# Seven instead of eight seven-product pairs in the second down projection of a decoder layer's first feed-forward block

## The chip, the cores and the metric

The kernel runs on one core of one Trainium2 chip. The metric is the time on the device in microseconds, from the launch of the program to its end; lower is better. A profiled execution gives, beside its own time, the span of the recorded instructions.

## The reference

One layer of a decoder, all in float32, for 256 tokens of width 2048. A feed-forward block (width 5632) stands before and behind a mixing stage of two head groups:

```python
def swiglu(x, w_gate, w_up, w_down):
    return (jax.nn.silu(x @ w_gate) * (x @ w_up)) @ w_down

def reference(x, ...):
    for l in range(DEPTH):          # DEPTH = 1
        x = x + 0.5 * swiglu(rms_norm(x, ffn1_norm[l]), ffn1_w_gate[l], ffn1_w_up[l], ffn1_w_down[l])
        h = rms_norm(x, mix_norm[l])
        z = h @ w_in[l]
        ...                         # gated linear attention and dilated attention
        x = x + jnp.concatenate([o_g, o_a], axis=-1) @ w_out[l]
        x = x + 0.5 * swiglu(rms_norm(x, ffn2_norm[l]), ffn2_w_gate[l], ffn2_w_up[l], ffn2_w_down[l])
    return x
```

The diff touches the last product of the first `swiglu`, the down projection: 256 x 5632 times 5632 x 2048.

## The kernel before, in words

**Precision.** TensorE multiplies fp32r numbers. Every float32 operand is split in two: a high part, which ScalarE copies (`split`, L115), and a low part, which VectorE subtracts (L116). A product is then three matmuls: high by high (L279 or L304), high by low weight (L281 or L305), low activation by high weight (L283 or L306). Each has a stationary block of 128 x 128 activations and streams 512 columns of weights.

**Columns, k-tiles and pairs.** The 2048 columns of the down projection's result are made in two goes of 1024 (`cp` 0 and 1); a go is called a column pair, or down pair here. It sums over 44 k-tiles of 128, taken two at a time as 22 k-pairs. The weights of a k-pair are one tile `raw` of 1 MB, one load on SP's queue (L221), with three buffers. The split weights `wh` and `wl` have four buffers each, and `weights()` prepares up to two tiles ahead of the one that it hands out.

**Plain and seven pairs.** A plain k-pair is two units, one for each k-tile: per unit two halves of the tokens, two halves of the columns and three matmuls, so 12, and 24 for the pair. Its weights are two splits of 128 x 1024. A seven pair computes the same 2 x 2 blocks (tokens) by 2 x 2 blocks (k by columns) with seven block products in place of eight, as Strassen's and Winograd's scheme does: 21 matmuls (`seven_products`). For that VectorE first adds up sums of the weight blocks (`seven`: L243, L244, L247) and splits them; its weights take three splits of 128 x 1024 and one of 128 x 512. It also needs sums of the activations (`seven_forms`: L322 twice, L325 to L328, a split), made once per k-pair and column pair where they are not kept from the column pair before. Plain products add into the banks `cs`, seven products into both `cs` and four more banks `ms`.

**The order.** `DOWN_ORDERS` holds for each column pair a text of 22 letters, s for plain and g for seven; `_order` numbers the seven pairs first, so that seven pairs are k-pairs 0, 1, 2 and so on. `seven_pair` walks through the units. Forms of the seven pairs 0 to 5 are made during the first column pair; those of 6 and 7 are made in the second one, at units 13 and 16 (`extra`), in rooms that pairs 1 and 2 have done with (`dforms`, parts of `hh` and `hl`). At the last seven pair the banks `ms` are folded into `xs` by nine instructions (`fold_into_xs`, L425 to L432), one for each following half unit (a half unit is one half of the tokens, 6 matmuls). At the end of a column pair `evac` adds the plain banks into `xs` (L531).

**Work beside it.** The list `later` holds small pieces of other work that are strewn over the half units. In the second down pair these are the norm for the mixing stage: finished columns are turned by VectorE (L130), moved by DMAs that POOL issues (L137), multiplied with the gains (L157) and split into `hh` and `hl`. While the rooms there are lent to the seven pairs, the pieces from L157 on wait in the list `held`, which joins `later` at the last seven pair:

```python
if n == lastseven:
    folds = fold([...])
    if holding[0] == 1:
        later.extend(held)
        held.clear()
        holding[0] = total = done = step = 0
        steps = 2 * (len(units) - n) - 6
```

A planner then orders each engine's instructions from this program by its own estimate of times, so that the queue of VectorE need not follow the text; in the trace some L157 run ahead of the last seven pair. Both layers' feed-forward blocks are made by the same function `ffn`; the second layer's (`final`) has no norm behind it.

Of the kernel before, what the change touches and what calls it, by code (L numbers as in the profile page):

```python
# [39 lines left out]
def _order(text):  # L40

    seven, plain = iter(range(text.count("g"))), iter(range(text.count("g"), len(text)))
    return [(next(seven), True) if c == "g" else (next(plain), False) for c in text]


FF_ORDERS = [_order("ssgsggss" if b in FF_THREE else "ssgssgss" if b in FF_SEVEN else "ssssssss") for b in range(FF // 512)]
DOWN_ORDERS = [_order("ssssssgssgssgsgsgsgsss"), _order("sgsgsgsgsgsgsgssgsssss")]
OUT_ORDERS = [_order("ssssssss"), _order("ssgsgsss")]


def layer_kernel(tc, x, xT, gains, gla_gate_up, gla_gate_bias, gla_out_norm, att_q_norm, att_k_norm,
# [6 lines left out]
    with ExitStack() as es:  # L58
# [7 lines left out]
        def acc_bank():  # L66
            n = order[0]
            order[0] = (n + 1) % 6
            if n < 4:
                return pacc.tile([P, 512], F32, name="acc", tag="acc")  # L70
            return paux.tile([P, 512], F32, name="acc", tag="acc")

        def four_banks(odd):

            if odd:
                return [paux.tile([P, 512], F32, name="acc", tag="acc") for _ in range(2)] + [tp_bank() for _ in range(2)]
            return [pacc.tile([P, 512], F32, name="acc", tag="acc") for _ in range(4)]

        def t512(name):
            return cst.tile([P, 512], F32, name=name, tag="t512", bufs=4)  # L80

        def tp_bank():
            return ptp.tile([P, 512], F32, name="tp", tag="tp")
# [11 lines left out]
        hh = cst.tile([P, KT, S], F32R, name="hh")  # L95
        hl = cst.tile([P, KT, S], F32R, name="hl")
# [80 lines left out]
        def jobs_of(w, orders):  # L177
            for cp, order in enumerate(orders):
                for kp, seven in order:
                    for part in ("plain", "last", "sums", "more") if seven else (0, 1):  # L180
                        yield w, cp * len(order) + kp, part

        jobs = [*jobs_of(w_ff1, FF_ORDERS), *jobs_of(w_dn1, DOWN_ORDERS)]
        jobs += [(w_mix, i, k) for i in range(3 * KT // 2) for k in range(2)] + ["low"]
        jobs += [(w_mix, i, k) for i in range(3 * KT // 2, 3 * KT) for k in range(2)]
        jobs += jobs_of(w_out, OUT_ORDERS)
        jobs += [*jobs_of(w_ff2, FF_ORDERS), *jobs_of(w_dn2, DOWN_ORDERS)]

        AHEAD = 2
        ready = []  # L190
# [68 lines left out]
        def weights(early=False):  # L259
            if early:  # L260
                return prepare()
            while jobs and len(ready) <= AHEAD:
                prepare()
            return ready.pop(0)
# [5 lines left out]
        def halves(a):  # L270
            return a.rearrange("p (b a) -> p b a", b=2)

        def products(ps, t, acts, ws, first, last, js=((0, 1),)):
            for jj in js:
                for i, ((ah, al, k), (wh, wl)) in enumerate(zip(acts, ws)):
                    sh = ah[:, k, t * P:(t + 1) * P]
                    sl = al[:, k, t * P:(t + 1) * P]
                    for j in jj:
                        nc.tensor.matmul(ps[j], lhsT=sh, rhs=alt(wh[:, j, :]), start=first and i == 0, stop=False)  # L279
                    for j in jj:  # L280
                        nc.tensor.matmul(ps[j], lhsT=sh, rhs=alt(wl[:, j, :]), start=False, stop=False)  # L281
                    for j in jj:
                        nc.tensor.matmul(ps[j], lhsT=sl, rhs=alt(wh[:, j, :]), start=False, stop=last and i == len(ws) - 1)  # L283
# [5 lines left out]
        def run_later(n):  # L289
            for _ in range(min(n, len(later))):  # L290
                later.pop(0)()
# [39 lines left out]
        def seven_pair(acts, pairs, forms, odd, evac, fold, span=None, final=False, extra=None):  # L331

            cs, ms, folds = [acc_bank(), acc_bank(), tp_bank(), tp_bank()] if odd is None else four_banks(odd), None, []
            if odd is not None:
                order[0] = 4 * (1 - odd)
            units = [u for kp, seven in pairs for u in ([kp] if seven else [(2 * kp,), (2 * kp + 1,)])]
            lastseven = max(n for n, u in enumerate(units) if not isinstance(u, tuple))  # L340
            steps = span or 2 * sum(isinstance(u, tuple) for u in units)
            total = done = step = n = 0
            while n < len(units):
                u = units[n]
                if extra and n in extra:
                    extra[n]()
                if isinstance(u, tuple):
                    g = WBUF if final and n == len(units) - WBUF else 1
                    ws = [weights() for _ in range(g)]
                    last = n + g == len(units)  # L350
                    for t in range(NT):
                        step += 1
                        total = max(total, done + len(later))
                        go = min(max(-(-total * min(step, steps) // steps) - done, 0), len(later))
                        done += go
                        run_later(go)
                        if folds:
                            folds.pop(0)()
                        now = [acts[v[0]] for v in units[n:n + g]]
                        products(cs[2 * t:2 * t + 2], t, now, ws, n == 0, last, ((0,), (1,)) if g > 1 else ((0, 1),))  # L360
                        if last:
                            evac(t, [c.rearrange("p (a b) -> p b a", b=2) for c in cs[2 * t:2 * t + 2]])
                    n += g
                    continue
                start = ms is None
                if start:
                    ms = [acc_bank() for _ in range(4)] if odd is None else four_banks(1 - odd)
                seven_products(cs, ms, acts[2 * u:2 * u + 2], forms[u], start, n == lastseven)
                if start:
                    later.extend(second)  # L370
                    second.clear()
                if n == lastseven:
                    folds = fold([m.rearrange("p (a b) -> p b a", b=2) for m in ms])
# [5 lines that stand above are left out]
                n += 1  # L379
# [37 lines left out]
        def lent(a, k, i):  # L417

            return a[:, k:k + 2, :].rearrange("p k (t q) -> p (k t) q", q=P) if i else a[:, k:k + 2, :].rearrange("p k s -> p (k s)").unsqueeze(1)
# [15 lines left out]
        def ffn(name, done, residual, extra=None, final=False):  # L435

            with tc.tile_pool(name=name, bufs=1, reuse_waits="tile") as fp:
# [8 lines left out]
                def part(k):  # L446
                    n = int(k >= tail)
                    return us_h[n], us_l[n], k - n * tail
# [59 lines left out]
                dacts = [part(k) for k in range(FT)]  # L508

                rooms["down"] = {"sum": urs, "wh": lent(hl, 8, 0), "wl": lent(hl, 10, 0)}  # L510
                dforms = {kp + 1: [lent(hh, 2 * kp, 1), lent(hl, 2 * kp, 1)] for kp in range(4)}
                dforms[0] = [lent(hh, 12, 1), lent(hh, 14, 1)]
                dforms[5] = [lent(hl, 12, 1), lent(hl, 14, 1)]
                dforms.update({6 + i: [lent(a, 2 * i, 1) for a in (hh, hl)] for i in range(2)})

                def sums_of(kp):
                    seven_forms(dacts[2 * kp:2 * kp + 2], dforms[kp], t512("full"), t512("sums"))

                rest, later[:] = later[:], []
                for step in range(32):  # L520
                    kp = step // 5 - 1
# [4 lines left out]
                for cp in range(2):  # L526
                    def evac(t, ps, cp=cp):
                        for j in range(2):
                            c = 2 * cp + j
                            blk = xs[:, t, c * 512:(c + 1) * 512]  # L530
                            nc.vector.scalar_tensor_tensor(halves(blk), ps[j], 0.5, halves(blk), op0=ALU.mult, op1=ALU.add)  # L531
                            done(t, c, blk)

                    def fold(m, cp=cp):
                        return fold_into_xs(m, cp, urs, 0.5)

                    holding[0] = NT - cp
                    seven_pair(dacts, DOWN_ORDERS[cp], dforms, cp, evac, fold, span=28 if cp else 32, final=final and cp == 1,
                               extra={13 + 3 * i: lambda kp=6 + i: sums_of(kp) for i in range(2)} if cp else None)
                spare.close()  # L540


# [457 lines left out]
```

## Time and profile before

| what | value |
|---|---|
| median of 3 runs | 1709.99 us (1709.28 to 1711.11) |
| profiled execution, its own time | 1710.49 us |
| profiled execution, span | 1708.7 us |
| TensorE busy | 1696.9 us, 7932 matmuls |
| VectorE busy | 1472.8 us |
| ScalarE busy | 973.4 us |
| GpSimd busy | 506.2 us |
| granted TensorE clock | 0.999 |

The engines' names in the profile are PE (TensorE matmul), PEld (TensorE weight load, which overlaps PE), DVE (VectorE), ACT (ScalarE), POOL (GpSimd) and SP. A row of the order of instructions gives the start, the duration, engine, line, operation, tile written and tiles read, shape and count, and in brackets how long the engine had been idle and what released it. A row of a group gives line, engine, operation, tiles, shape and count, then the busy time in us and the mean of one in ns, then the idle time before them. The second down pair of the first layer runs from about 560 to 672 us of the span, that of the second layer from about 1594 to the end.

### The profile page before, as it was taken

The numbers are of one execution on the slowest core, as the hardware profiler recorded it, in microseconds if no ns is written. First come the engines' busy times: TensorE is split into PE (matmuls) and PEld (weight loads), VectorE is DVE, ScalarE is ACT, GpSimd is POOL, SyncE is SP. The second block draws the span as 40 slices with busy tenths as digits, with TensorE's granted clock in tenths as the row PEclk, the third lists the DMA queues.
The fourth block names the chain that finished last, engine by engine and source line by source line (L and its number), as shares of the span: only waits on it lengthen the run. The fifth ranks groups of instructions, "written<-read, shape, count | busy, mean of one in ns | idle before, by whom it ended". The sixth has DMA issues, their size and how long they took to land.

```text
span 1708.7 us, 22402 instructions
## 1 busy us (share of the span) xinstructions
PE 1696.9 (99%) x7932; PEld 1477.4 (86%) x7932; DVE 1472.8 (86%) x1823; ACT 973.4 (57%) x1207; POOL 506.2 (30%) x1002
## 2 busy tenths in 40 slices
PE   9999999999999999999999999999999999999999
PEld 7888888888888878888888888888888888888887
DVE  6989999999899997577856688989998999899986
ACT  7656565555555555564654555556555655555553
POOL 0333334343400601064250034333333333420000
PEclk9999999999999999999999999999999999999999
DMA  8566656666666666567564457666666666666663
GB/s 347 211 232 225 218 210 236 212 235 216 235 245 223 216 220 226 195 231 243 190 217 169 151 198 249 231 234 210 235 224 229 223 215 219 222 247 232 220 235 135
DMA packets 85809, 378.63 MB, mean 222 GB/s; under 512 B 21393, under 2 KB 38801, under 8 KB 42689
## 3 DMA queue, kind: packets, MB, share of 16 engines
q1 hardware_dynamic: 50864, 350.25, 57.9%
q0 software_dynamic: 34112, 25.88, 5.4%
q8 instruction: 62, 1.02, 0.2%
q10 hardware_dynamic: 720, 1.07, 0.2%
q14 instruction: 51, 0.41, 0.1%
HBM read 354.57 MB, written 4.19 MB: 210 GB/s over the span
## 4 chain that ended last, share of the span: by engine, by line
PE 89%; DVE 5%; DMA 4%; issue 1%; POOL 0%; ACT 0%; DVEq 0%; SPq 0%; ACTq 0%; POOLq 0%
PE acc L281 19%; PE acc L283 19%; PE acc L279 19%; PE acc L305 5%; PE acc L306 5%; PE acc L304 5%; PE tp L283 4%; PE tp L281 4%; PE tp L279 4%; DVE wl L116 3%; DMA raw<-in_w_dn_dram 2%; PE tp L306 1%; PE tp L305 1%; PE tp L304 1%; DMA xs<-us 1%
## 5 line engine op out<-in xcount | busy, mean ns | idle before, releaser
L115 ACT ACTIVATE wh<-raw 128x1024 fp32r<-128x1024 f32 (+2 forms) x610 | 631.9, 1047 | 444.0 <-PE acc L283 207.0
L116 DVE TENSOR_TENSOR wl<-raw,wh 128x1024 fp32r<-128x1024 f32 (+1 forms) x608 | 733.1, 1215 | 127.0 <-ACT wh L115 124.3
L137 POOL DMA_DIRECT2D xs<-us x704 | 344.5, 497 | 545.6 <-DVE us L130 284.1
L283 PE MATMUL acc<-wh,hl 128*128 128x512 f32 x1192 | 359.3, 381 | 0.0
L281 PE MATMUL acc<-wl,hh 128*128 128x512 f32 x1192 | 358.8, 381 | 0.1
L279 PE MATMUL acc<-wh,hh 128*128 128x512 f32 x1192 | 347.9, 381 | 2.3 <-ACT wh L115 2.3
L279 PEld LDWEIGHTS acc<-wh,hh 128*128 128x128 f32 x1192 | 224.8, 189 | 35.4 <-ACT wh L115 3.5
L281 PEld LDWEIGHTS acc<-wl,hh 128*128 128x128 f32 x1192 | 225.1, 189 | 32.7 <-DVE wl L116 0.5
L283 PEld LDWEIGHTS acc<-wh,hl 128*128 128x128 f32 x1192 | 225.3, 189 | 32.2 <-issue 0.5
L115 ACT ACTIVATE wh<-xs 128x1024 fp32r<-128x1024 f32 x100 | 105.6, 1056 | 103.3 <-DVE xs L247 31.9
L116 DVE TENSOR_TENSOR wl<-xs,wh 128x1024 fp32r<-128x1024 f32 x100 | 120.4, 1214 | 2.7 <-ACT wh L115 2.6
L281 PE MATMUL acc<-wl,uh 128*128 128x512 f32 x368 | 113.1, 381 | 2.6 <-DVE wl L116 2.6
L283 PE MATMUL acc<-wh,ul 128*128 128x512 f32 x368 | 112.2, 379 | 0.0
L279 PE MATMUL acc<-wh,uh 128*128 128x512 f32 x368 | 106.2, 380 | 0.5 <-ACT wh L115 0.5
L137 POOL DMA_DIRECT2D hh<-us x128 | 62.1, 500 | 121.1 <-DVE xs L531 68.5
L243 DVE TENSOR_TENSOR xs<-raw 128x1024 f32<-128x1024 f32 x50 | 61.1, 1222 | 29.3 <-DMA raw<-in_w_ff_dram 29.2
L281 PEld LDWEIGHTS acc<-wl,uh 128*128 128x128 f32 x368 | 68.7, 189 | 15.1 <-DVE wl L116 5.6
L279 PEld LDWEIGHTS acc<-wh,uh 128*128 128x128 f32 x368 | 69.3, 189 | 11.1 <-ACT wh L115 1.3
L283 PEld LDWEIGHTS acc<-wh,ul 128*128 128x128 f32 x368 | 69.6, 189 | 9.9
L279 PE MATMUL tp<-wh,hh 128*128 128x512 f32 x200 | 61.6, 379 | 0.0
L281 PE MATMUL tp<-wl,hh 128*128 128x512 f32 x200 | 59.5, 379 | 0.0
L283 PE MATMUL tp<-wh,hl 128*128 128x512 f32 x200 | 59.5, 379 | 0.0
(326 smaller groups left out, 2540.0 us busy)
## 6 DMA issues: line engine op xcount, KB each, us to landing
raw<-in_w_ff_dram SPq DMA_DIRECT2D x175, 1024.0 KB, 5.1
raw<-in_w_dn_dram SPq DMA_DIRECT2D x88, 1024.0 KB, 4.9
raw<-in_w_mix_dram SPq DMA_DIRECT2D x48, 1024.0 KB, 5.0
raw<-in_w_out_dram SPq DMA_DIRECT2D x16, 1024.0 KB, 4.8
xs<-us POOLq DMA_DIRECT2D x704, 16.0 KB, 4.0
xs<-in_x_dram SPq DMA_DIRECT2D x2, 1024.0 KB, 9.5
xs<-in_x_dram POOLq DMA_DIRECT2D x2, 1024.0 KB, 5.9
hh<-us POOLq DMA_DIRECT2D x128, 16.0 KB, 3.7
```

What stands on the lines that cost most here:

```text
L115: nc.scalar.activation(dst_h, src, AF.Copy)
L116: nc.vector.tensor_sub(dst_l, src, dst_h.bitcast(F32))
L137: nc.gpsimd.dma_start(dst[32 * q:32 * q + 32, ..., r * n:(r + 1) * n], src[32 * r:32 * r + 32, ..., q * n:(q + 1) * n])
L243: nc.vector.tensor_add(room["sum"], b1, blocks[:, 1:3, :])
L279: nc.tensor.matmul(ps[j], lhsT=sh, rhs=alt(wh[:, j, :]), start=first and i == 0, stop=False)
L281: nc.tensor.matmul(ps[j], lhsT=sh, rhs=alt(wl[:, j, :]), start=False, stop=False)
L283: nc.tensor.matmul(ps[j], lhsT=sl, rhs=alt(wh[:, j, :]), start=False, stop=last and i == len(ws) - 1)
L304: nc.tensor.matmul(bank, lhsT=a[0], rhs=alt(ws[0][:, j, :]), start=start, stop=False)
L305: nc.tensor.matmul(bank, lhsT=a[0], rhs=alt(ws[1][:, j, :]), start=False, stop=False)
L306: nc.tensor.matmul(bank, lhsT=a[1], rhs=alt(ws[0][:, j, :]), start=False, stop=stop)
```

## The change

The first layer's second down pair gets an order of its own. Before, both layers had `sgsgsgsgsgsgsgssgsssss`: eight seven pairs, mostly with one plain pair between two of them, and five plain pairs behind the last. Now the first layer has `sgsgssgssgssgssgssgsss`: seven seven pairs, the first two one plain pair apart, the others two, and three plain pairs behind the last. The units become 37 instead of 36, and the last seven pair is unit 30 instead of 25. The forms of k-pair 7 are no longer made in the first layer, since it is plain. The first down pair of both layers and everything of the second layer keep their text. The loop around the folds runs once, as the statement without it did.

```diff
-DOWN_ORDERS = [_order("ssssssgssgssgsgsgsgsss"), _order("sgsgsgsgsgsgsgssgsssss")]
+DOWN_ORDERS = {name: [_order("ssssssgssgssgsgsgsgsss"), _order(text)]
+               for name, text in (("ffn1", "sgsgssgssgssgssgssgsss"), ("ffn2", "sgsgsgsgsgsgsgssgsssss"))}
...
-        jobs = [*jobs_of(w_ff1, FF_ORDERS), *jobs_of(w_dn1, DOWN_ORDERS)]
+        jobs = [*jobs_of(w_ff1, FF_ORDERS), *jobs_of(w_dn1, DOWN_ORDERS["ffn1"])]
...
-        jobs += [*jobs_of(w_ff2, FF_ORDERS), *jobs_of(w_dn2, DOWN_ORDERS)]
+        jobs += [*jobs_of(w_ff2, FF_ORDERS), *jobs_of(w_dn2, DOWN_ORDERS["ffn2"])]
...
-                        if folds:
-                            folds.pop(0)()
+                        for _ in range(1):
+                            if folds:
+                                folds.pop(0)()
...
-                dforms.update({6 + i: [lent(a, 2 * i, 1) for a in (hh, hl)] for i in range(2)})
+                dforms.update({6 + i: [lent(a, 2 * i, 1) for a in (hh, hl)] for i in range(3)})
...
-                    seven_pair(dacts, DOWN_ORDERS[cp], dforms, cp, evac, fold, span=28 if cp else 32, final=final and cp == 1,
-                               extra={13 + 3 * i: lambda kp=6 + i: sums_of(kp) for i in range(2)} if cp else None)
+                    seven_pair(dacts, DOWN_ORDERS[name][cp], dforms, cp, evac, fold, span=28 if cp else 32, final=final and cp == 1,
+                               extra={at: lambda kp=6 + i: sums_of(kp) for i, at in enumerate((13,16,) if final else (13,))} if cp else None)
```

## The prediction

> **What bounds the kernel now.** I read the page first, then the engines' busy time by stretches, then the waits and the order of instructions around the second down pair of the first layer (called the stage below).
>
> ```profile
> span 1708.7 us, 22402 instructions
> PE   1696.9 (99%) x7932; PEld 1477.4 (86%) x7932; DVE 1472.8 (86%) x1823; ACT 973.4 (57%) x1207; POOL 506.2 (30%) x1002
> PE 89%; DVE 5%; DMA 4%; issue 1%; POOL 0%; ACT 0%; DVEq 0%; SPq 0%; ACTq 0%; POOLq 0%
> ```
>
> TensorE (PE) carries 89% of the chain that ended last, VectorE (DVE) 5%. So time falls by fewer matmuls, or by taking away a place where PE waits for weights. The change adds matmuls, so only waits are to be won. The stretches show whether the stage has any. Its ends are two like instructions: the first L531 after the pair before it, and the first L531 at its own end. Each was released by the same point of a pair (the first half of the tokens of its last k-tile), so the distance between them is one whole pair. The columns of the rows that begin with a stretch are its length and the busy time of PE, PEld, DVE, ACT and POOL, with clock, DMA share and GB/s last.
>
> ```profile
> 559.82 0.69 DVE L531 SCALAR_TENSOR_TENSOR xs<-acc,xs 128x512 f32<-128x512 f32 x1 [0.42 <-PE acc L283]
> 672.04 0.69 DVE L531 SCALAR_TENSOR_TENSOR xs<-acc,xs 128x512 f32<-128x512 f32 x1 [1.36 <-PE acc L283]
> 559.80:672.00 112.20, 109.82 (x505) 94.85 (x505) 99.44 (x118) 62.65 (x74) 35.50 (x72) 1.00 0.67 223
> 600.00:640.00 40.00, 37.62 (x171) 31.64 (x170) 37.43 (x45) 22.27 (x26) 1.72 (x4) 1.00 0.62 220
> 640.00:672.00 32.00, 32.00 (x150) 28.03 (x149) 23.79 (x27) 15.96 (x17) 4.44 (x8) 1.00 0.71 243
> 1600.00:1640.00 40.00, 40.00 (x187) 35.04 (x186) 34.88 (x37) 24.77 (x27) 0.00 (x0) 1.00 0.60 213
> ```
>
> PE is idle for 2.38 us between 600 and 640 and nowhere else in the stage, at a granted clock of 1.00 throughout. The last row is the same place of the second layer, whose second down pair runs the same order of pairs: no idle time. What PE waited for:
>
> ```profile
> 601.74 0.30 PEld L281 LDWEIGHTS acc<-wl,uh 128*128 128x128 f32 x2 [1.14 <-DVE wl L116]
> 612.82 0.30 PEld L281 LDWEIGHTS acc<-wl,uh 128*128 128x128 f32 x2 [1.51 <-DVE wl L116]
> 623.34 0.30 PEld L281 LDWEIGHTS acc<-wl,uh 128*128 128x128 f32 x2 [0.93 <-DVE wl L116]
> 633.32 0.30 PEld L281 LDWEIGHTS acc<-wl,uh 128*128 128x128 f32 x2 [0.40 <-DVE wl L116]
> ```
>
> Four times, some 10.5 us apart (one seven pair with one plain pair), PE stands before the low part of a plain k-tile's weights, which VectorE has not subtracted yet. VectorE is 37.43/40 = 94% busy there; in the second layer 34.88/40 = 87%.
>
> **What the waits cost in full.** I count matmuls against the pitch of the undisturbed end of the stage.
>
> ```profile
> 659.11 0.59 PE L279 MATMUL tp<-wh,uh 128*128 128x512 f32 x2
> 669.47 0.59 PE L279 MATMUL tp<-wh,uh 128*128 128x512 f32 x2
> ```
>
> Between these two rows lie four k-tiles of 12 matmuls: 10.36/48 = 0.2158 us each. The stage has 14 plain pairs of 24 matmuls and 8 seven pairs of 21: 504, or 108.78 us without waits. It took 672.04 - 559.82 = 112.22. So the waits cost 3.44 us, more than the 2.38 of idle PE, since the matmuls around a wait are also further apart. A second way gives the same. The first addition of the folded products into xs (L427) comes after the same work in both layers:
>
> ```profile
> 645.97 0.68 DVE L427 SCALAR_TENSOR_TENSOR xs<-urs,xs 128x512 f32<-128x512 f32 x1
> 1593.69 0.69 DVE L531 SCALAR_TENSOR_TENSOR xs<-acc,xs 128x512 f32<-128x512 f32 x1 [0.29 <-PE acc L283]
> 1676.48 0.69 DVE L427 SCALAR_TENSOR_TENSOR xs<-urs,xs 128x512 f32<-128x512 f32 x1
> 559.80:645.90 86.10, 83.72 (x384) 71.99 (x384) 80.34 (x97) 49.68 (x61) 31.06 (x64) 1.00 0.63 208
> 1593.70:1676.40 82.70, 82.61 (x382) 71.52 (x381) 72.01 (x75) 47.76 (x51) 0.00 (x0) 1.00 0.62 220
> ```
>
> First layer 645.97 - 559.82 = 86.15, second 1676.48 - 1593.69 = 82.79: 3.36 us apart, for the same matmuls. VectorE did 80.34 - 72.01 = 8.3 us more in the first: it turns and normalizes the finished columns for the next stage (the four L130 and four L157 below, with their splits).
>
> The Trainium skill (Perfetto Trace Analysis, section Identifying the Most-Contended Engine) says that matmul busy time is a poor measure and weight-load busy time a good one. By idle PE alone the waits cost 2.38 us; by weight loads, from 600 to 640, (35.04 - 31.64) x 40/35.04 = 3.88. With either in the sum below the forecast would move by -1.1 or +0.4 us of gain; the evacuation rows stand between them, nearer the rule.
>
> **The change part by part.**
>
> ```profile
> L116 DVE TENSOR_TENSOR wl<-raw,wh 128x1024 fp32r<-128x1024 f32 x44 | 53.0, 1219 | 8.8 <-ACT wh L115 8.7
> L243 DVE TENSOR_TENSOR urs<-raw 128x1024 f32<-128x1024 f32 x7 | 8.6, 1223 | 2.6 <-DMA raw<-in_w_dn_dram 2.6
> L116 DVE TENSOR_TENSOR hl<-raw,hl 128x512 fp32r<-128x512 f32 x7 | 4.8, 685 | 0.0
> L244 DVE TENSOR_TENSOR raw<-urs,raw 128x512 f32<-128x512 f32 x7 | 4.8, 684 | 0.0
> L247 DVE TENSOR_TENSOR raw<-raw 128x512 f32<-128x512 f32 x7 | 4.8, 684 | 0.0
> L157 DVE TENSOR_TENSOR hf<-hh,gT 128x512 f32<-128x512 f32 x4 | 2.7, 685 | 0.0
> L116 DVE TENSOR_TENSOR hl<-hf,hh 128x512 fp32r<-128x512 f32 x4 | 2.7, 684 | 0.0
> L130 DVE STREAM_TRANSPOSE us<-xs 128x512 f32<-128x512 f32 x4 | 2.7, 695 | 0.0
> L322 DVE TENSOR_TENSOR full<-uh,ul 128x256 f32<-128x256 f32 x4 | 1.5, 410 | 0.0
> ```
>
> - One pair of 22 turns from seven to plain: 24 - 21 = 3 more matmuls, 3 x 0.2158 = +0.65 us, all on the path.
> - Its weights: a seven pair takes VectorE one L243 (1.22), L244, L247 and the single block's subtraction (0.68 each) and three subtractions of 1.22, in all 6.93 us; a plain pair two of 1.22, 2.44. That is 4.5 us less VectorE, and one and a half ACT splits less. Both kinds load one raw tile, so the DMA queue of SP issues the same 22 loads.
> - The forms of the eighth seven pair go (the extra at unit 16): two L322 (0.82), four small ones and a split, some 2.6 us of VectorE and one ACT instruction. Together VectorE loses 7.1 us: 99.44 becomes 92.3 in 109.4 us, 84%, under the 87% at which the second layer loses nothing, though it now carries the norm work too.
> - The spacing. A seven pair with one plain pair has 9.37 us of VectorE in 45 matmuls (9.7 us), 96%. With two plain pairs it is 11.8 in 69 (14.9), 79%, so that each group has 3 us to spare for the norm work. Only the first two seven pairs stay one plain pair apart, and up to 600, for almost four groups, PE did not wait (below).
> - The seventh seven pair's forms are made at unit 13 as before, in a room whose first user ran at unit 5; no cost.
>
> ```profile
> 561.00:600.00 39.00, 39.00 (x183) 34.14 (x182) 37.04 (x47) 23.95 (x32) 29.34 (x61) 1.00 0.69 211
> 672.00:1490.00 818.00, 818.00 (x3886) 713.43 (x3885) 676.58 (x856) 464.83 (x624) 279.96 (x538) 1.00 0.63 215
> ```
>
> - The loop over one fold per step runs once, as before: nothing. The second layer's order is the same text: nothing.
> - The end is tighter: after the last seven pair come 6 plain k-tiles, not 10. In 72 matmuls, 15.5 us, VectorE must finish the folds, the held norms must write their split into hh (the room of the last seven pair's forms, so not earlier), and the held work is spread over 8 steps, not 16. This cost is in no row; below is how I bound it.
>
> ```profile
> 655.85 0.68 DVE L432 TENSOR_TENSOR urs<-urs,acc 128x512 f32<-128x512 f32 x1
> 658.01 1.06 ACT L115 ACTIVATE wh<-raw 128x1024 fp32r<-128x1024 f32 x1 [1.53 <-PE tp L283]
> 659.10 1.23 DVE L116 TENSOR_TENSOR wl<-raw,wh 128x1024 fp32r<-128x1024 f32 x1 [0.23 <-ACT wh L115]
> ```
>
> From the first fold addition (645.97) VectorE needed 13.1 us until it waited for ScalarE again (659.10), with folds, two held splits and the running weights done. 13.1 is under 15.5, so I take nothing. The banks of the folds, which the next stage starts with, are read last by L432, 9.9 us after the first addition; also in time. At the worst all four L157 and the two other splits fall there as well: 6 x 0.685 = 4.1 more, 17.2, a lag of 1.7 us. There ScalarE refills a weight tile as soon as PE frees it; with four tiles, each 2.59 us of matmuls, a new one is ready 3 x 2.59 - 1.06 - 1.23 = 5.5 us before its use. So the bounds are 0 and, for the unknown, the 3.44 of the stage; I take 0, since the lag does not reach the cushion.
>
> **Sum.** 0.65 - 3.44 = -2.79 at best; I leave 0.2 us of waits in place, about half of the smallest one above. From the profiled execution's 1710.49 that is 1707.9. That run lies 0.50 above the median 1709.99, so as a median 1707.4. After the stage PE has no idle time up to 1490 (the row above), so nothing is there to swallow the gain.
>
> **The rivals.**
>
> *Half the waits stay.* The planner that orders VectorE's queue may place norm work just ahead of needed weights, as at 600. Half of 3.44 left: 1.72 - 0.65 = 1.1 us won, 1708.9.
>
> *The raw buffers are the limit, not VectorE.* VectorE waited 2.6 us for raw loads in this stage (the L243 row), just ahead of the late weights. Then every seven pair from the fourth on keeps its wait: three of four, 3.44/4 - 0.65 = 0.2 us won, 1709.8. The Trainium skill (Perfetto Trace Analysis, section Optimization Strategy) says that a gap that repeats can mean too few buffers, which speaks for this one. Against it stands the second layer:
>
> ```profile
> DVE urs L243 <- DMA raw<-in_w_dn_dram: 9.0, 6, 2.4
> ```
>
> In 1593 to 1676 VectorE waited 9.0 us for such loads, with the same three buffers, and PE lost nothing.
>
> *Slower: the end of the stage.* The folds and held norms, squeezed into 12 steps, leave VectorE behind when the next stage begins with its own norm work, and PE waits there. It must lag 5.5 us to be felt, 5.5 + 2.8 = 8.3 to lose the whole gain, and 5.5 + 2.8 + 3.4 = 11.7 for slower by 0.2%; I find 1.7 at the worst. It would give 1710 to 1714.
>
> *More than the cap.* Other stages reorder in its favour, or the runs scatter (1709.28 to 1711.11 shown): below 1706.6.
>
> **How the numbers follow.** 0.2%, about what a measurement of this kernel can tell from no change, is 3.4 us: below 1706.6 is faster, above 1713.4 slower. Forecast 0.65, half the waits 0.13, buffers 0.09, end of the stage 0.07 (0.05 of it slower by 0.2%), more than the cap 0.06. Scatter lifts another 0.06 of the forecast's share over the line. So faster 0.12, same 0.83, slower 0.05. The forecast's own range is 1706.4 to 1708.3; with the half case and the buffers 1706.4 to 1709.9 holds some 8 in 10.
>
> **What would show it.** Right: the distance between the two L531 is near 109.5 us; no PE or weight-load wait on wl L116 of more than 0.3 us in the stage; PE has 7935 matmuls; VectorE is some 7 us less busy; the next stage starts without idle PE. Wrong: waits that come again with each seven pair (buffers), or PE idle in the first 20 us of the mixing stage (the squeezed end), or lost time in a stage that the diff does not touch.

## The result, and the profile after

| | before | after |
|---|---|---|
| median, runs beside each other | 1711.11 us (22 runs, 1709.28 to 1715.58) | 1707.38 us (22 runs, 1706.70 to 1710.82) |
| ratio | | 0.998, 95% interval 0.9974 to 0.9986 |
| profiled execution, its own time | 1710.49 us | 1707.46 us |
| the stage, L531 to L531 (after: L533) | 112.22 us | 109.43 us |

The changed kernel is faster by 2.4 to 4.4 us, about 0.2%, just at the line that the prediction drew. The lines of the changed kernel are one or two higher: L531 is now L533, L116 is L117, L243 is L244, L427 is L429. The page of the changed kernel, the ends of its stage, and its stretches (length, then busy time of PE, PEld, DVE, ACT, POOL):

```profile
span 1705.7 us, 22393 instructions
PE   1696.8 (99%) x7935; PEld 1478.6 (87%) x7935; DVE 1467.1 (86%) x1811; ACT 972.3 (57%) x1204; POOL 505.4 (30%) x1002
```

```profile
559.66 0.69 DVE L533 SCALAR_TENSOR_TENSOR xs<-acc,xs 128x512 f32<-128x512 f32 x1 [0.20 <-PE acc L284]
669.09 0.69 DVE L533 SCALAR_TENSOR_TENSOR xs<-acc,xs 128x512 f32<-128x512 f32 x1 [1.35 <-PE acc L284]
```

```profile
559.80:669.20 109.40, 109.40 (x509) 95.80 (x508) 93.58 (x107) 62.12 (x71) 35.50 (x72) 1.00 0.67 224
600.00:640.00 40.00, 40.00 (x187) 35.01 (x187) 34.97 (x40) 22.47 (x24) 1.94 (x4) 1.00 0.57 201
640.00:672.00 32.00, 32.00 (x150) 28.03 (x149) 26.88 (x31) 17.52 (x21) 4.43 (x8) 1.00 0.72 245
```

TensorE is busy for all of the stage. Between 600 and 640, where it had been idle for 2.38 us, VectorE is now 34.97/40 = 87% busy instead of 94%. The stage is 112.22 - 109.43 = 2.79 us shorter; the two spans differ by 1708.7 - 1705.7 = 3.0. The other 0.2 lies ahead of the stage, which begins 0.16 us earlier; from the end of the stage to the end of the span it is 1036.7 us before and 1036.6 after.

VectorE's waits in the two stages (before in the first fence, after in the second):

```profile
DVE wl L116 <- ACT wh L115: 8.7, 8, 1.4
DVE urs L243 <- DMA raw<-in_w_dn_dram: 2.6, 4, 1.0
```

```profile
DVE urs L244 <- DMA raw<-in_w_dn_dram: 9.5, 5, 2.3
DVE wl L117 <- ACT wh L116: 4.8, 8, 1.0
```

VectorE waits longer for raw loads than before, 9.5 us against 2.6, while TensorE waits no longer at all: these waits cost nothing here. They do not tell by themselves whether VectorE is ahead or behind, because almost every load is issued only when VectorE has finished with an older tile. In the stage before the change SP's queue waited 21 times for VectorE's subtractions (L116), 98.7 us in all.

### The profile page after: what moved, and what is told of

It reads as the page before. It is cut to its first block, busy times and chain, and to the rows that moved or that the text cites. A ratio compares the mean times of both kernels' runs of the same rounds, so it can differ in the third digit from the quotient of the medians.

```text
span 1705.7 us, 22393 instructions
## 1 busy us (share of the span) xinstructions
PE 1696.8 (99%) x7935; PEld 1478.6 (87%) x7935; DVE 1467.1 (86%) x1811; ACT 972.3 (57%) x1204; POOL 505.4 (30%) x1002
## 4 chain that ended last, share of the span: by engine, by line
PE 92%; DVE 4%; DMA 2%; issue 1%; ACT 0%; POOL 0%; DVEq 0%; ACTq 0%; SPq 0%; POOLq 0%
PE acc L282 19%; PE acc L284 19%; PE acc L280 19%; PE acc L306 5%; PE acc L307 5%; PE acc L305 5%; PE tp L284 4%; PE tp L280 4%; PE tp L282 4%; DVE wl L117 2%; PE tp L307 1%; PE tp L306 1%; PE tp L305 1%; DMA raw<-in_w_ff_dram 1%; DMA xs<-us 1%
## 5 line engine op out<-in xcount | busy, mean ns | idle before, releaser
L116 ACT ACTIVATE wh<-raw 128x1024 fp32r<-128x1024 f32 (+2 forms) x610 | 632.4, 1048 | 429.1 <-PE acc L284 206.2
L117 DVE TENSOR_TENSOR wl<-raw,wh 128x1024 fp32r<-128x1024 f32 (+1 forms) x608 | 733.0, 1214 | 123.0 <-ACT wh L116 120.0
L284 PE MATMUL acc<-wh,hl 128*128 128x512 f32 x1192 | 359.5, 381 | 0.0
L284 PEld LDWEIGHTS acc<-wh,hl 128*128 128x128 f32 x1192 | 225.3, 189 | 32.3 <-issue 0.5
L116 ACT ACTIVATE wh<-xs 128x1024 fp32r<-128x1024 f32 x100 | 105.6, 1056 | 105.1 <-DVE xs L248 33.3
L117 DVE TENSOR_TENSOR wl<-xs,wh 128x1024 fp32r<-128x1024 f32 x100 | 120.3, 1212 | 4.2 <-ACT wh L116 4.2
L284 PE MATMUL acc<-wh,ul 128*128 128x512 f32 x372 | 113.4, 379 | 0.0
L244 DVE TENSOR_TENSOR xs<-raw 128x1024 f32<-128x1024 f32 x50 | 61.0, 1221 | 27.6 <-DMA raw<-in_w_ff_dram 27.5
L284 PEld LDWEIGHTS acc<-wh,ul 128*128 128x128 f32 x372 | 70.3, 189 | 10.0
L284 PE MATMUL tp<-wh,hl 128*128 128x512 f32 x200 | 59.5, 379 | 0.0
```

Of the source, the lines that this page charges most:

```text
L116: nc.scalar.activation(dst_h, src, AF.Copy)
L117: nc.vector.tensor_sub(dst_l, src, dst_h.bitcast(F32))
L244: nc.vector.tensor_add(room["sum"], b1, blocks[:, 1:3, :])
```

## The experiments

The theory is that of the prediction: VectorE's work in groups of one seven and one plain pair leaves no room for the norm work, and TensorE waits for late low parts. The rivals are that the number of seven pairs alone decides, and that the three raw buffers are the limit. The runs of one kernel scatter over 3 to 9 us, the effects in dispute are 0.65 to 3.4 us, so I read the stage in each profile, from the first L531 (L533) that TensorE released to the next, and put the time beside it. The ratios are to the kernel before in the same series of runs; they weigh all runs and need not be the quotient of the medians. Where VectorE still had work queued at an end of the stage the row shows no releaser, and the distance is then only a bound.

**The changed kernel again.** No edit.

> The changed kernel again, beside the others. Theory (VectorE is overloaded in the stage, the change relieves it): the stage, from the first evacuation row of the first column pair to that of the second, 109.4 us with no wait of TensorE; time 2.8 to 3.7 us under the kernel before. If the excess of the medians over the 2.79 us of the stage is real and not scatter, the difference comes out near 3.7 again.

> The changed kernel once more, as the partner of the next run. Theory: stage 109.4 us, no wait in it; its runs fall in a lower and an upper group some 3 to 6 us apart, as before.

The first gave a median of 1710.17 us (11 runs) beside 1711.49 of before, ratio 0.9988 (0.9979 to 0.9998); the second 1707.68 (10 runs) beside 1710.62, ratio 0.9987 (0.9975 to 0.9999). Stage of the second: 669.21 - 559.78 = 109.43. Differences of 1.3 and 2.9 us stand beside the 3.7 of the first comparison, and the 2.79 us of the stage lies inside the interval of all three. The excess over it did not come again in the first and hardly in the second, which speaks for scatter. In the second series eight runs lay from 1706.88 to 1708.55 us and two at 1712.63 and 1716.29, so the two groups were there, further apart than expected. The last section shows what made the first one's profiled execution 6.5 us longer than its lowest run.

**Without the norm work (e3).** The edit is made in the kernel before the change.

```diff
-            to.append(lambda: (norm_moved if c < 2 else norm_block)(t, c, gi))
+            if c >= 2 or gi != 1:
+                to.append(lambda: (norm_moved if c < 2 else norm_block)(t, c, gi))
```

> The kernel before the change, but the norm of the first 1024 columns for the mixing stage is left out (four L130, their DMAs, four L157 and four splits; the mixing stage then reads what is in hh). VectorE's load falls by some 8 us in the stage, order of pairs and raw buffers as before. Theory VectorE: no wait left, stage 108.8 us, time 3.4 us under the kernel before. Rival raw buffers: waits with each seven pair from the fourth on stay, stage 111 to 112, time within 1 us of before.

In the order of instructions the ends of the stage, then the stretch with its busy times, then VectorE's wait for loads among the waits of the stage:

```profile
562.59 0.69 DVE L531 SCALAR_TENSOR_TENSOR xs<-acc,xs 128x512 f32<-128x512 f32 x1
671.37 0.69 DVE L531 SCALAR_TENSOR_TENSOR xs<-acc,xs 128x512 f32<-128x512 f32 x1 [1.36 <-PE acc L283]
```

```profile
559.00:672.00 113.00, 113.00 (x525) 98.97 (x524) 94.32 (x101) 64.47 (x72) 4.41 (x8) 1.00 0.63 221
```

```profile
DVE urs L243 <- DMA raw<-in_w_dn_dram: 8.1, 6, 2.3
```

Same order of pairs, same eight seven pairs, same raw buffers: no wait of TensorE, 108.78 us, just the 504 x 0.2158 of the prediction. (The first row shows no releaser, but TensorE has no idle time from 559 to 672 either.) The raw buffers and the number of seven pairs as sole causes fall, since both were left as they were. The norm's small DMAs are gone with it, so VectorE's work alone is tested by the additions further down, not here. The time followed only in part: 1710.59 us, ratio 0.9993 (0.9984 to 1.0002). The profiled execution was the longest of its ten, 1712.77 us. In it the stage begins 2.8 us later: the granted clock was 0.98 in the first 100 us against 1.00, and TensorE was idle for 1.52 us from 480 to 510, 0.82 before. From 1490 to 1590 it was idle for 2.24 us, 0.52 before. The planner had ordered other stages anew too; which part of that is the edit's and which is scatter is not settled.

**The number alone (e1):** seven seven pairs, one plain pair apart. (Below the diff and the expectation stand the ends of the stage and TensorE's waits, in order of time; so in the later ones.)

```diff
-("ffn1", "sgsgssgssgssgssgssgsss")
+("ffn1", "sgsgsgsgsgsgsgssssssss")
```

> Seven seven pairs as in the change, but each one plain pair apart and eight plain pairs behind the last (sgsgsgsgsgsgsgssssssss): the number alone. Theory of VectorE's load in place: the groups from the fourth on wait as before the change, 2.5 to 3.4 us of waits, stage 112 to 113 us, time about that of the kernel before. Rival that the number decides (one seven pair's VectorE work less is the cure): stage near 109.4.

```profile
559.55 0.69 DVE L533 SCALAR_TENSOR_TENSOR xs<-acc,xs 128x512 f32<-128x512 f32 x1 [0.32 <-PE acc L284]
601.07 0.70 PE L282 MATMUL acc<-wl,uh 128*128 128x512 f32 x2 [0.34 <-DVE wl L117]
612.08 0.70 PE L282 MATMUL acc<-wl,uh 128*128 128x512 f32 x2 [1.03 <-DVE wl L117]
671.27 0.69 DVE L533 SCALAR_TENSOR_TENSOR xs<-acc,xs 128x512 f32<-128x512 f32 x1 [1.36 <-PE acc L284]
```

The waits at 601 and 612 are there again. Stage 111.72, so 111.72 - 109.43 = 2.29 us of waits remain of 3.44, a little under the range expected. Time as before the change: 1711.12 us, ratio 1.0 (0.999 to 1.001).

**The spacing alone (e2 and e8):** eight seven pairs, spread in two ways. (The first leaves out the last of the nine folds.)

```diff
-("ffn1", "sgsgssgssgssgssgssgsss")
+("ffn1", "sgssgsgssgsgssgsgssgss")     # e2
+("ffn1", "sgsgsgssgssgsgssgsgsss")     # e8
...
-extra={at: lambda kp=6 + i: sums_of(kp) for i, at in enumerate((13,16,) if final else (13,))}
+extra={at: lambda kp=6 + i: sums_of(kp) for i, at in enumerate((13, 16))}     # both
```

> Eight seven pairs as before the change, but spread evenly (one and two plain pairs apart in turn, two plain pairs behind the last... the text of the order is sgssgsgssgsgssgsgssgss). Folds may be one short of steps there, which concerns the sum in xs and no other instruction. Theory of VectorE's load in place (groups of one plain pair at 96% of VectorE are what PE waits behind): most waits go, the stage takes 108.8 to 109.8 us, time 0 to 0.7 us under the changed kernel. Rival that the number of seven pairs decides (8 x 6.93 + forms are too much wherever they stand): the waits stay near 3.4 us, stage 112, time as before the change.

> Eight seven pairs, the first three one plain pair apart as before, the later ones spread (sgsgsgssgssgsgssgsgsss), three plain pairs behind the last. Theory of load in place: the early tight groups cost nothing, as before the change up to 600 us; later waits mostly gone, stage 108.8 to 109.6, time up to 0.65 us under the changed kernel. Rival number: stage near 112.

The busy times of the first's stretch and, from the order of instructions, its idle TensorE; then the second's ends and its one wait, with the row of VectorE ahead of it:

```profile
559.00:672.00 113.00, 112.04 (x517) 97.11 (x516) 100.93 (x120) 64.88 (x76) 35.53 (x72) 1.00 0.66 219
```

```profile
609.87 0.48 PE L306 MATMUL acc<-wl,hh 128*128 128x512 f32 x1 [0.23 <-DVE wl L117]
637.46 0.70 PE L282 MATMUL acc<-wl,uh 128*128 128x512 f32 x2 [0.58 <-DVE wl L117]
```

```profile
559.38 0.69 DVE L533 SCALAR_TENSOR_TENSOR xs<-acc,xs 128x512 f32<-128x512 f32 x1 [0.22 <-PE acc L284]
642.39 1.23 DVE L244 TENSOR_TENSOR urs<-raw 128x1024 f32<-128x1024 f32 x1 [1.49 <-DMA raw<-in_w_dn_dram]
644.80 0.48 PE L306 MATMUL acc<-wl,hh 128*128 128x512 f32 x1 [1.28 <-DVE wl L117]
669.72 0.69 DVE L533 SCALAR_TENSOR_TENSOR xs<-acc,xs 128x512 f32<-128x512 f32 x1 [1.35 <-PE acc L284]
```

The second keeps 110.34 - 108.78 = 1.56 us of waits, at the seventh of its eight seven pairs. The first ends with VectorE behind, so I count there from matmul to matmul: the last two L284 of the first column pair begin at 560.70, those of the second at 671.24. That is 110.54 us, 1.76 of them waits; idle TensorE is 0.96 us. Both expectations were too low: eight seven pairs still wait when well spread, and e8's stage is 0.9 us longer than the changed kernel's in spite of three matmuls fewer. Times: 1711.20 us, ratio 0.9996 (0.9987 to 1.0006), and 1709.28, ratio 0.9985 (0.9976 to 0.9995). The changed kernel beside them stood at 1710.17, so these times do not rank the three; the stages do.

In e8 the late weights stand right behind a wait of VectorE for a raw load, and e8 is not alone in this. Two rows of VectorE's queue before the change, ahead of TensorE's wait at 612.82, then two of e1, ahead of its wait at 612.08:

```profile
610.41 1.23 DVE L243 TENSOR_TENSOR urs<-raw 128x1024 f32<-128x1024 f32 x1 [0.77 <-DMA raw<-in_w_dn_dram]
611.55 1.22 DVE L116 TENSOR_TENSOR wl<-raw,wh 128x1024 fp32r<-128x1024 f32 x1
```

```profile
609.66 1.23 DVE L244 TENSOR_TENSOR urs<-raw 128x1024 f32<-128x1024 f32 x1 [2.15 <-DMA raw<-in_w_dn_dram]
610.81 1.22 DVE L117 TENSOR_TENSOR wl<-raw,wh 128x1024 fp32r<-128x1024 f32 x1
```

VectorE stood idle for 0.77 and 2.15 us before an addition whose load had not landed, and the subtraction that TensorE needed next came behind that addition. So TensorE's wait is not made of VectorE's work alone. As each load had waited for VectorE in its turn, a late VectorE makes a late load, and the load holds VectorE up again. A fourth raw buffer was not tried, so how much of the waits it would take away stays open.

**More work on VectorE in the changed kernel (e5).**

```diff
                 seven_products(cs, ms, acts[2 * u:2 * u + 2], forms[u], start, n == lastseven)
+                if len(pairs) == 22 and odd == 1 and not final and u >= 2:
+                    for _ in range(3):
+                        nc.vector.tensor_add(t512("idle"), rooms["down"]["sum"][:, 0, :], rooms["down"]["sum"][:, 0, :])
```

> The changed kernel with three additions of 128x512 more on VectorE (0.68 us each, into a tile that nobody reads) behind each of the last five seven pairs, 10 us in all: each group then has some 15 us of VectorE in 14.9 us of matmuls. Order, raw buffers and products stay. Theory VectorE: waits on wl come back, 1 to 4 us, stage 110.5 to 113.5 us. Rival (the spacing gives the raw buffers time, VectorE is not the limit): stage 109.4 to 109.8.

```profile
560.12 0.59 PE L284 MATMUL acc<-wh,ul 128*128 128x512 f32 x2
642.34 1.22 DVE L244 TENSOR_TENSOR urs<-raw 128x1024 f32<-128x1024 f32 x1 [2.33 <-DMA raw<-in_w_dn_dram]
649.50 0.70 PE L282 MATMUL acc<-wl,uh 128*128 128x512 f32 x2 [0.40 <-DVE wl L117]
654.17 0.48 PE L306 MATMUL acc<-wl,hh 128*128 128x512 f32 x1 [0.53 <-DVE wl L117]
657.65 0.70 PE L282 MATMUL acc<-wl,uh 128*128 128x512 f32 x2 [0.62 <-DVE wl L117]
672.00 0.59 PE L284 MATMUL tp<-wh,ul 128*128 128x512 f32 x2
```

The ends of the stage are here the last L284 of the two column pairs, since VectorE was behind at the last L536. With the order of the change and its buffers, more work on VectorE alone brings waits back: 672.00 - 560.12 - 109.43 = 2.45 us, 1.55 of it as idle TensorE. They come late. VectorE stood 2.33 us for a raw load at 642.34 and was then busy without a pause, with the added work, norm pieces and weights one behind another, while TensorE waited three times. Whether the work acts directly or by later loads, this run does not separate. Time 1710.06 us, ratio 0.9997 (0.9988 to 1.0007).

**A shorter end (e6).** All seven seven pairs two plain pairs apart, two plain pairs behind the last, two folds per step in this column pair.

```diff
-("ffn1", "sgsgssgssgssgssgssgsss")
+("ffn1", "sgssgssgssgssgssgssgss")
...
-                        for _ in range(1):
+                        for _ in range(2 if len(pairs) == 22 and span == 28 and not final else 1):
```

> Seven seven pairs, all two plain pairs apart, so that only two plain pairs (4 units, 48 matmuls, 10.4 us) stand behind the last (sgssgssgssgssgssgssgss); two folds per step there. This squeezes the end of the stage further. My price of the end: VectorE needs 13.1 us for folds and weights, so it lags 2.7 us into the mixing stage, below the cushion of 5.5 us: no wait of TensorE there, stage 109.4, time as the changed kernel. Rival (the end is dear): TensorE idle for 1 us or more between 668 and 690.

```profile
559.15 0.69 DVE L533 SCALAR_TENSOR_TENSOR xs<-acc,xs 128x512 f32<-128x512 f32 x1 [0.29 <-PE acc L284]
670.29 1.28 DVE L533 SCALAR_TENSOR_TENSOR xs<-acc,xs 128x512 f32<-128x512 f32 x2
```

```profile
559.00:672.00 113.00, 113.00 (x525) 98.97 (x524) 97.00 (x110) 64.34 (x76) 35.46 (x72) 1.00 0.68 224
672.00:700.00 28.00, 28.00 (x139) 24.64 (x139) 20.85 (x34) 14.43 (x20) 3.80 (x4) 1.00 0.62 217
```

TensorE should release the last evacuation at 559.15 + 109.43 = 668.58; VectorE comes to it at 670.29, so it lags 1.7 us (2.7 expected), and TensorE is not idle in the stage or the next 28 us. The cushion carries it. Time 1707.53 us, ratio 0.998 (0.9968 to 0.9993): as the change.

**One seven pair fewer still (e7).**

```diff
-("ffn1", "sgsgssgssgssgssgssgsss")
+("ffn1", "sgssgssgssgssgssgsssss")
...
-extra={at: lambda kp=6 + i: sums_of(kp) for i, at in enumerate((13,16,) if final else (13,))}
+extra={at: lambda kp=6 + i: sums_of(kp) for i, at in enumerate((13, 16) if final else ())}
```

> One step further in the same direction: six seven pairs, two plain pairs apart, five plain pairs behind the last (sgssgssgssgssgssgsssss). Theory: no waits are left to win, three more matmuls cost 0.65 us: stage 110.1 us, time 0.65 us over the changed kernel. Rival (VectorE still holds TensorE back somewhere near): stage at or below 109.4.

```profile
561.49 0.69 DVE L533 SCALAR_TENSOR_TENSOR xs<-acc,xs 128x512 f32<-128x512 f32 x1 [0.42 <-PE acc L284]
671.57 0.69 DVE L533 SCALAR_TENSOR_TENSOR xs<-acc,xs 128x512 f32<-128x512 f32 x1 [1.36 <-PE acc L284]
```

110.08 us: 0.65 more than 109.43, three matmuls. With no wait left, plain pairs only cost. Time 1708.93 us, ratio 0.999 (0.9981 to 0.9999).

**The stores of the residual on another queue (e9).** An attempt on the scatter of the runs.

```diff
-extra={9 + t: lambda t=t: nc.gpsimd.dma_start(resid[t * P:(t + 1) * P, :], xs[:, t, :]) for t in range(NT)}
+extra={9 + t: lambda t=t: nc.sync.dma_start(resid[t * P:(t + 1) * P, :], xs[:, t, :]) for t in range(NT)}
```

> The changed kernel with the two 1 MB stores of the residual before the second layer (L926) issued on SP's queue, not POOL's. In one profile of the changed kernel one of these stores took 13.0 us, VectorE stood 4.0 us before its first L323 in the second layer (it overwrites what the store still reads), and TensorE 3.5 us. Theory (the spread of the changed kernel's runs comes from that place): the store lands sooner or no later than 9 us, the upper group of runs gets thinner, median 0 to 3 us under the changed kernel beside it; the stage stays 109.4. Rival (the spread comes from the start of the program or elsewhere): same spread and median.

The stores landed in 4.7 us (median of the two), 7.5 in the changed kernel beside it, but the median was 1709.37 us (1708.21 to 1714.24) against 1707.68 (1706.88 to 1716.29), and the lowest run was 1.3 us higher. One of its eleven runs still stood over 1712 us, two of ten beside it, too few to call the upper end thinner. So that place explains one long run, the profiled one; what made the others stays open, as does the extra microsecond.

No kernel here beat the changed one by more than the scatter.

## Why the prediction was right

- *The waits' full price.* 3.44 us by the two evacuation rows was exact: without norm work the same pairs take 108.78. Idle TensorE (2.38) was too low and the weight loads (3.88) somewhat too high, so the rule cited from the Trainium skill pointed the right way, though its page speaks of how near a kernel is to roofline and not of the price of waits; the distance between like rows was better than both. The reason that the prediction gives for the missing 1.06 us covers less than half of it: a pair of matmuls behind a wait has a row of 0.70 us in place of 0.59, 0.1 at each of four waits. The rest is that a matmul's row lasts 0.38 us against a pitch of 0.2158, so the row ahead of each wait hides 0.17 us of it.
- *The cost of the plain pair.* 0.65 us forecast; 0.65 measured from seven to six seven pairs.
- *Spacing and number.* I named both without saying how much each carries. Number alone left 2.29 us of 3.44, spacing alone 1.76 (e2) and 1.56 (e8); only together nothing.
- *The 0.2 us left in place.* None was left: the stage took 109.43, the 109.43 of 112.22 - 2.79. From the profiled 1710.49 the full sum gives 1707.70, and the execution took 1707.46.
- *VectorE's saving.* Mis-sized: 7.1 us forecast, 1472.8 - 1467.1 = 5.7 measured. I added durations; neighbouring instructions overlap, and start to start one of 128x1024 takes 1.13 to 1.14 us, not 1.22. Over the 12 instructions fewer that is about 1 of the 1.4 us; the rest is open. The same slip is in the 96% of the spacing: the second layer ran such groups without norm work at 87%. So such groups by themselves leave room, as e3 shows too; they are too much only together with the norm work. The time did not depend on the size of the saving.
- *The tight end.* Right, and with room: from the first fold addition to VectorE's next wait for ScalarE it took 666.51 - 652.81 = 13.7 us in the changed kernel (13.1 before), under the 15.5 there, and in e6 the cushion held a real lag.

```profile
652.81 0.68 DVE L429 SCALAR_TENSOR_TENSOR xs<-urs,xs 128x512 f32<-128x512 f32 x1
666.51 1.23 DVE L117 TENSOR_TENSOR wl<-raw,wh 128x1024 fp32r<-128x1024 f32 x1 [0.80 <-ACT wh L116]
```

- *Half the waits stay* and *raw buffers* did not come about here; e1 and e8 are what the first looks like. But the prediction set VectorE and the buffers against each other too sharply. Its 2.6 us of load waits stood just ahead of the late weights at two of the four places only (0.48 and 0.77 us); ahead of the other two VectorE had waited for ScalarE (0.60 and 1.20 us). Loads and VectorE hold each other up, as e1 and e8 show.
- The median came out as 1707.38 against 1707.4, and that closeness is luck: the before beside it stood at 1711.11, not 1709.99. The difference of medians, 3.7 us, is more than the forecast 2.6; repeats gave 1.3 and 2.9.

## What to carry to other kernels

Where a helper engine has almost no idle time for long (here 94 to 95% busy from 561 to 640 us, with waits only from 601 on), a cheaper algorithm on TensorE (seven products for eight) can cost more there in waits than it saves; price both, 0.65 us a pair against the waits that one group makes. Measure waits by the distance between two like instructions against the pitch of an undisturbed stretch, and look for the same code elsewhere in the program without the extra work. A helper's wait for loads is no sign of too few buffers while the main engine does not wait (9.5 us here). Where it stands right ahead of the main engine's wait, as in e1 and e8, it is part of that wait; then ask what released the load.

## What the runs showed of the hardware

One execution of the changed kernel took 1713.56 us. Its stage was as good as the others'. In the second layer one of the two stores of the residual took 13.0 us to land (8.8 at most for these stores and the loads that read them back in the first profile of the change), and VectorE, next in whose queue stood an instruction that overwrites the stored data, kept everything behind it waiting. Order of instructions, then stretches with the granted clock in the third column from the right:

```profile
1063.79 0.76 DVE L323 TENSOR_TENSOR xs<-hh,hl 128x256 f32<-128x256 f32 x2 [3.97 <-DMA resid<-xs]
1065.74 1.22 PE L282 MATMUL acc<-wl,hh 128*128 128x512 f32 x2 [3.54 <-DVE wl L117]
```

```profile
1062.00:1065.70 3.70, 0.20 (x1) 0.00 (x0) 1.91 (x4) 0.89 (x1) 0.00 (x0) 0.89 0.19 78
1065.70:1071.70 6.00, 5.96 (x14) 4.79 (x15) 6.00 (x11) 1.69 (x2) 0.00 (x0) 0.50 0.57 188
1071.70:1074.00 2.30, 2.30 (x12) 2.00 (x12) 2.18 (x7) 0.63 (x1) 0.00 (x0) 0.99 0.87 353
```

TensorE had no matmul for 3.54 us, and then ran at half the clock for 6 us: 14 matmuls where 28 fit. So the one wait cost 3.5 + 3 us, as much as the 6.5 us by which this run stood over the lowest beside it (1707.06). The Trainium skill (TensorE: Matmul & The Clock Gate, Part 1) says that the clock halves after an idle window of about 3.4 us. The trace agrees that one gap of this kind halves it, but shows the fall earlier: a mean of 0.89 over the 3.70 us of the first row puts it 0.8 us before the next matmul, 2.7 us after the last one. The waits in the stage, at most 1.28 us of idle TensorE (e8), left the clock at 1.00.
